# A decoder layer on one core: every on-chip tile is moved to byte 0 of a 256-byte line

## The chip, the cores and the metric

The kernel runs on one core of one Trainium2 chip. Its time is the device time of one execution in microseconds. The kernel before took 1461.62 us (median of 3 runs, 1461.08 to 1461.69).

## The reference

One decoder layer for 512 tokens of 1024 features, in float32:

```
x <- x + 1/2 * SwiGLU(RMSNorm(x))                       first FFN, 1024 -> 2 x 2816 -> 1024
h  = RMSNorm(x);  P = h @ W_in                          one projection for all mixers
branch A: sparse attention, 16 heads x 64 (compressed, selected, sliding window)
branch B: short gated convolution, 1024 channels
branch M: cross-attention into 256 memory tokens, 4 heads x 256
x <- x + W_out( sig(gA)*A + sig(gB)*B + sig(gM)*M )
x <- x + 1/2 * SwiGLU(RMSNorm(x))                       second FFN, same shapes
```

With 512 tokens every key block is selected and the window holds all earlier tokens, so the two large branches of A are causal attentions over 512 keys.

## The kernel before, in words

Activations stand as features on the 128 partitions and tokens on the free axis. Every product is done in float32r with both operands split exactly into two parts, hi and lo; `mm3` (L194 to L199) issues three matmuls for each product of tiles, at L197 (hi, hi), L198 (hi weights, lo activations) and L199 (lo weights, hi activations). Each matmul loads a stationary operand of 128 columns (512 bytes per partition) and streams a moving operand, in most cases of 512 columns (2048 bytes per partition).

Weights come from DRAM in units of up to 128x1024 float32 (`Weights`, from L58): SyncE issues a load into one of three `wraw` buffers, ScalarE rounds a half into `whi` (L93), VectorE takes the rest into `wlo` (L94), each with two buffers, one unit ahead of the use.

The stages follow each other on TensorE:

- First FFN (`ffn`, L258 to L309), in three groups of 8, 7 and 7 blocks of 128 hidden features. Each group first does its up-projections (two units per block, each 8 x 3 = 24 matmuls: stationary `whi` or `wlo`, moving `Ahi` or `Alo`, out to PSUM `psg` and `pso`), then its down-projection (8 units of 24 or 21 matmuls: stationary `whi`/`wlo`, moving `ghi`/`glo`, out to `pss`). So an up group has 8 x 48 = 384 or 7 x 48 = 336 long matmuls, a down group 192 or 168.
- Keys and values of the memory (`mem_kv`): 192 long matmuls, stationary `mhi`/`mlo`, moving `whi`/`wlo`.
- Token-major projections (`tok_chunk`, `stage_b`): stationary `Ahi`/`Alo`, moving `whi`/`wlo`, 512 columns wide in six chunks of 96 matmuls, 304 and 256 wide in two more, with the compression and the attention over the memory set between them. In the latter (`mem_head`) the values `Vm` are stationary and the probabilities `mph`/`mpl` move, twelve matmuls in a row per head.
- Eight rounds (`feat_quanta`, `att_quanta`), each 144 long matmuls for the convolution and the merge gates (stationary `whi`/`wlo`, moving `Ahi`/`Alo`), in bursts of nine, and between the bursts the transposes, scores and value products of the attention.
- The output projection (`tail`, L1161 on): 192 long matmuls, moving `Ahi`/`Alo`; then the second FFN through the same `ffn`, with `x2hi`/`x2lo` in place of `Ahi`/`Alo`.

The program is written in this order; the order of the instructions on each engine comes from the order of the closures that `interleave` (L44) sets among each other. On-chip memory is taken from pools, stacked from the left or the right end; in a pool each tile starts where the one before it ended, rounded up to 32 bytes. So where a tile begins follows from the sizes of those ahead of it: `small` (412 bytes) begins at byte 128 of a 256-byte line, and what follows it is shifted by what remains. In the built program the tiles that TensorE reads begin at these bytes (the address per partition, and its remainder by 256):

| Tile | Before: address, byte in line | After: address, byte in line |
|---|---|---|
| Ahi; Alo | 33856, 64; 50240, 64 | 34304, 0; 50688, 0 |
| whi (two buffers) | 80224, 96; 84320, 96 | 80640, 0; 84736, 0 |
| wlo (two buffers) | 88416, 96; 92512, 96 | 88832, 0; 92928, 0 |
| ghi; glo, first FFN | 107936, 160; 124320, 160 | 108544, 0; 124928, 0 |
| mhi; mlo | 168640, 192; 176832, 192 | 168192, 0; 176384, 0 |
| Vm (first); mph, heads 0 and 1 | 204768, 224; 188384, 224 | 204544, 0; 188160, 0 |
| V2; PThi (first) | 154784, 160; 204640, 96 | 155392, 0; 204032, 0 |
| x2hi; x2lo | 96608, 96; 112992, 96 | 97024, 0; 113408, 0 |
| ghi; glo, second FFN | 137568, 96; 153952, 96 | 137984, 0; 154368, 0 |

Slices of these tiles that a long matmul reads lie whole multiples of 512 bytes from the tile's start, so the remainder by 256 is the same for all of a tile's matmuls.

Of the kernel before, what the change touches and what calls it, by code (L numbers as in the profile page):

```python
# [11 lines left out]
F32 = mybir.dt.float32  # L12
# [12 lines left out]
EPS = 1e-6  # L25
NEG8 = -8e30
TW = 528
WL = 656
BUCKET_START = (0, 1, 2, 3, 4, 5, 6, 7, 8, 9, 10, 11, 12, 13, 14, 15,
                16, 19, 21, 24, 27, 31, 35, 40, 46, 52, 59, 67, 77, 87, 99, 113)  # L30
RAW_BUFS = 3
LOOK = 1

# columns of the per-feature constants
# [3 lines left out]
# chunks of projections with tokens on partitions: columns, and k tiles of each unit  # L38
# [5 lines left out]
def interleave(main, aux):  # L44
    """Emit the closures of aux evenly between those of main."""
    n, done = len(main), 0
    for i, fn in enumerate(main):
        fn()
        want = (i + 1) * len(aux) // n
        while done < want:  # L50
            aux[done]()
            done += 1
    while done < len(aux):
        aux[done]()
        done += 1


class Weights:  # L58
    """Streams weight units from DRAM and splits them exactly into two float32r parts."""
# [18 lines left out]
    def _half(self):  # L78
        """Split one half of the next unit."""
        j = self.i_split  # L80
        t, n = self.raw[j]
        if j not in self.parts:
            hi = self.pool.tile([128, 1024], F32R, tag="whi", name=f"whi{j}", bufs=LOOK + 1)
            lo = self.pool.tile([128, 1024], F32R, tag="wlo", name=f"wlo{j}", bufs=LOOK + 1)
            self.parts[j] = (hi, lo)
            c = slice(0, min(n, 512))
        else:
            c = slice(512, n)
        if c.stop == n:
            self.raw.pop(j)  # L90
            self.i_split += 1
        hi, lo = self.parts[j]
        self.nc.scalar.copy(hi[:, c], t[:, c])  # L93
        self.nc.vector.tensor_sub(lo[:, c], t[:, c], hi[:, c].bitcast(F32))  # L94
        self.prefetch()
# [5 lines left out]
    def use(self, key):  # L101
        """The next unit; its key must be the one expected here. Begins to split the one after it."""
        assert self.units[self.i][1] == key, (self.units[self.i][1], key)
        self.prefetch()
        while self.i_split <= self.i:
            self._half()
        self.i += 1
        self.ahead()
        return self.parts[self.i - 1]

    def ahead(self):
        """Split another half of the unit after the one in use (called in the middle of a unit)."""
        self.parts.pop(self.i - 2, None)
        if self.i_split < len(self.units) and self.i_split <= self.i + LOOK - 1:
            self._half()


class Layer:
    def __init__(self, ctx, tc, ins, out, dbg=None):
# [3 lines left out]
        self.per = ctx.enter_context(tc.tile_pool(name="per", bufs=1, side="left"))  # L123
        self.wp = ctx.enter_context(tc.tile_pool(name="wp", bufs=1, side="left"))
        self.psum = ctx.enter_context(tc.tile_pool(name="ps", bufs=2, space=bass.MemoryType.PSUM))
        self.dram = ctx.enter_context(tc.tile_pool(name="dr", bufs=1, space=bass.MemoryType.DRAM))
        self.ws = Weights(nc, self.wp, self.unit_list())

# [65 lines left out]
    def mm3(self, ps, ahi, alo, bhi, blo, start, stop):  # L194
        """ps (+)= a.T @ b, each operand in its two exact parts."""
        mm = self.nc.tensor.matmul
        mm(ps, ahi, bhi, start=start, stop=False)  # L197
        mm(ps, ahi, blo, start=False, stop=False)  # L198
        mm(ps, alo, bhi, start=False, stop=stop)  # L199

    def rsqrt(self, pool, v, n, out, p=128):
        """out = v ** -0.5 over [p, n]: an estimate from the exponent bits, then Newton's steps."""
# [10 lines left out]
    def rstd(self, pool, ssq, n, width, out):  # L213
        """out = rsqrt(ssq / width + EPS) over [128, n]."""
# [4 lines left out]
    def token_rstd(self, pool, acc, nb, out):  # L219
        """acc [128 features, 128*nb tokens], squares already summed over feature tiles -> out [128 tok, nb]."""  # L220
        p = self.ps("t")
# [4 lines left out]
    def bcast_rows(self, rs, R):  # L226
        """R[m, t] = rs[t] for every partition m; rs is [128 tok, 4]."""
# [5 lines left out]
    def split_scaled(self, hi, lo, src, scale):  # L233
        """hi, lo = the exact parts of src * scale (scale per partition)."""
# [7 lines left out]
    def prep_post(self, pool, k, src, gcol, hi, lo, acc):  # L242
        """Parts of src * gain for a product scaled by rstd afterwards, and the running sum of squares."""
# [3 lines left out]
    def square_sum(self, pool, k, src, acc):  # L247
        """acc (+)= src ** 2"""
# [9 lines left out]
    def ffn(self, key, pool, xhi, xlo, R, done, before, extra=()):  # L258
        """done(m, ps): takes the last partial product (times 4 of what is to be added to x).
        before(): emitted after the first two products, which do not need R; extra: closures  # L260
        emitted one by one after the following ones."""
# [50 lines left out]
    def run(self):  # L312
# [20 lines left out]
        # the engines' first use, while the first loads run  # L333
# [11 lines left out]
        for h in (1, 0):  # L345
            mkp[h] = memkv[h].enter_context(tc.tile_pool(name=f"mkp{h}", bufs=1, side="right"))
        prep = ExitStack()
        pp = prep.enter_context(tc.tile_pool(name="pp", bufs=1, side="right"))
        f1 = ExitStack()
        fp = f1.enter_context(tc.tile_pool(name="fp", bufs=1, side="left"))  # L350

        # first ffn
# [24 lines left out]
        # h = rmsnorm(x1), under the product of the memory's keys and values  # L377
# [15 lines left out]
        # mixing phase  # L393
        mx1 = ExitStack()
        self.m1 = mx1.enter_context(tc.tile_pool(name="m1", bufs=1, side="left"))
# [8 lines left out]
    def bias_table(self, pool):  # L404
# [18 lines left out]
        def repeat(h, n):  # L423
            # a head's row once per query of a block, so that a pitch of WL - 1 shifts it by one
# [25 lines left out]
    def mem_kv(self, pools, pp, aux):  # L450
        """Emits the product; returns the closures that finish the keys."""
# [64 lines left out]
    def tok_chunk(self, c, evac):  # L516
        """Closures for one chunk of columns; evac(tb, ps) takes each block of 128 tokens."""
# [21 lines left out]
    def stage_b(self, memkv, prep, kfin):  # L539
# [7 lines left out]
        # inputs of the compression, while the memory's keys are finished  # L547
        kcs = ExitStack()
        kcv = kcs.enter_context(tc.tile_pool(name="kcs", bufs=1, side="left")).tile([128, 4, 512], F32, name="kcv")
# [5 lines left out]
        cp = cs.enter_context(tc.tile_pool(name="cp", bufs=1, side="right"))  # L555
# [30 lines left out]
        # keys and values of the selected and the window branch, with the memory's attention  # L586
        self.mx2 = ExitStack()
        m2 = self.mx2.enter_context(tc.tile_pool(name="m2", bufs=1, side="left"))
# [3 lines left out]
        pool = ma.enter_context(tc.tile_pool(name="ma0", bufs=1, side="right"))  # L592
# [5 lines left out]
        kp = kx.enter_context(tc.tile_pool(name="kp", bufs=1, side="left"))  # L598
# [26 lines left out]
        pool = ma.enter_context(tc.tile_pool(name="ma1", bufs=1, side="right"))  # L625
# [5 lines left out]
        # queries  # L631
        self.rx = ExitStack()
        self.tp = self.rx.enter_context(tc.tile_pool(name="tp", bufs=1, side="right"))
# [43 lines left out]
        # the first heads' scores, under the last chunk of queries  # L677
        self.rp = self.rx.enter_context(tc.tile_pool(name="rp", bufs=1, side="right"))
# [23 lines left out]
    def key_parts(self, dst, src):  # L702
        """dst rows 0..63 the high, rows 64..127 the low parts of the keys (src holds them in both halves)."""
# [12 lines left out]
    def compress(self, cp, kcv, kind):  # L716
# [7 lines left out]
        def trans(gp):  # L724
# [6 lines left out]
            # token = 16 * c + 2 * q + parity  # L731
# [93 lines left out]
    def mem_heads(self, pool, qtok, mrsq, heads):  # L825
        """Closures of the heads' attention, each head's second half among the next one's first."""
# [12 lines left out]
    def mem_head(self, pool, qtok, mrsq, h):  # L839
# [19 lines left out]
        def score(i2):  # L859
            if i2 == 0:  # L860
                st["P"] = pool.tile([128, 4, 256], F32, tag="mP", name=self.nm("mP"))
                st["sum"] = pool.tile([128, 4], F32, tag="msum", name=self.nm("msum"))
                st["nm"] = pool.tile([128, 4], F32, tag="mnm", name=self.nm("mnm"))
# [14 lines left out]
        def norm():  # L878
            r = pool.tile([128, 4], F32, tag="mr", name=self.nm("mr"))
# [29 lines left out]
    def q_norm(self, h):  # L909
        """The head's normalised queries, twice side by side."""  # L910
# [21 lines left out]
    def softmax_part(self, s, T, P, nm, ssum):  # L932
        """P = exp(score - max), its sum in ssum; the score is s / 8 + T / 8."""
# [39 lines left out]
    def probs(self, b, part):  # L973
        """Scale by gate / sum, in two parts."""
# [32 lines left out]
    def pv(self):  # L1007
        """The product of the last transposed block with its values."""
# [38 lines left out]
    def combine(self):  # L1047
        """Add the two halves of a finished head's output: rows 0..63 the main, 64..127 the low part."""
# [112 lines left out]
    def tail(self, mx1):  # L1161
# [12 lines left out]
        fp = f2.enter_context(tc.tile_pool(name="fp2", bufs=1, side="left"))  # L1174
# [35 lines left out]
def layout(i):  # L1210
    """The arrays as the kernel reads them: elements moved and copied, nothing computed from them."""
# [4 lines left out]
    def feat(w, n):  # L1216
        """[128 p, k * 128 + col] blocks of a [K, 128 * n] matrix."""
# [3 lines left out]
    def tok(w):  # L1221
        """Units of two k tiles and 512 columns of a [1024, 512 * n] matrix."""
# [3 lines left out]
    def units(w, kts):  # L1226
        """Units of some k tiles each of a [1024, n] matrix, side by side on 128 partitions."""
# [57 lines left out]
```

## Time and profile before

| What | Value |
|---|---|
| Time, median of 3 runs | 1461.62 us |
| Span of the profiled execution | 1460.0 us |
| TensorE (PE) busy | 1448.8 us, 99% |
| VectorE (DVE) busy | 888.6 us, 61% |
| ScalarE (ACT) busy | 633.5 us, 43% |
| DMA engines, mean in the first FFN and in the rounds | 0.37 and 0.24 of their time |

The profile shows each matmul with a start and a modelled end. Matmuls overlap: a long one is shown with some 390 to 400 ns, while the next begins some 230 ns after it. What TensorE needs for a stretch of matmuls is therefore read from starts: the length of a stretch in which it never idles, divided by the matmuls in it. A stretch's count includes those that reach into it from before. Times below count from the span's start.

### The profile page before, as it was taken

How to read it: one execution, taken by the hardware profiler on the slowest of the kernel's cores; microseconds unless marked ns; L12 is line 12 of the kernel's file. 1: busy time of each engine (PE TensorE's matmuls, PEld its weight loads, DVE VectorE, ACT ScalarE, POOL GpSimd, SP SyncE). 2: the span in 40 equal slices, each digit the busy share in tenths (PEclk: the TensorE clock that was granted, in tenths of full speed). 3: DMA queues.
4: the chain of work that ended last, by engine and by line, in shares of the span. 5: the costliest groups of instructions: out<-in, count | busy, mean ns of one | idle time of the engine just before them, and what ended most of it. 6: DMA issues, size and time to landing. Idle time of an engine off the chain costs nothing.

```text
span 1460.0 us, 18864 instructions
## 1 busy us (share of the span) xinstructions
PE 1448.8 (99%) x6915; PEld 1199.6 (82%) x6915; DVE 888.6 (61%) x2120; ACT 633.5 (43%) x1455; POOL 1.3 (0%) x8
## 2 busy tenths in 40 slices
PE   9999999999999999999999999999999999999998
PEld 7788888888887789878888888888888888888887
DVE  6463544454676566688777787877755444454553
ACT  5241322233555555565566566556533222322321
POOL 0000000000000000000000000000000000000000
PEclk9999999999999999999999999999999999999999
DMA  5733233333452421222222222221233332333332
GB/s 178 245 119 102 87 96 92 102 85 90 138 178 75 149 93 57 89 80 66 88 66 75 76 69 73 70 84 58 72 102 87 101 94 95 101 90 100 99 92 96
DMA packets 42892, 142.62 MB, mean 98 GB/s; under 512 B 4704, under 2 KB 4992, under 8 KB 42672
## 3 DMA queue, kind: packets, MB, share of 16 engines
q1 hardware_dynamic: 40320, 134.83, 29.8%
q10 hardware_dynamic: 2480, 6.60, 1.3%
q8 instruction: 54, 0.88, 0.2%
q14 instruction: 38, 0.31, 0.1%
HBM read 139.27 MB, written 7.51 MB: 101 GB/s over the span
## 4 chain that ended last, share of the span: by engine, by line
PE 96%; DVE 2%; ACT 1%; issue 1%; DMA 0%; SPq 0%; ACTq 0%
PE psg L197 15%; PE psg L198 15%; PE psg L199 15%; PE pso L197 7%; PE pso L199 7%; PE pso L198 7%; PE pss L198 6%; PE pss L199 6%; PE pss L197 6%; PE pst L1001 2%; PE pss L959 1%; PE pso L1025 1%; PE pss L958 1%; PE pso L1024 1%; PE pst L926 1%
## 5 line engine op out<-in xcount | busy, mean ns | idle before, releaser
L93 ACT CAST whi<-wraw 128x512 fp32r<-128x512 f32 (+1 forms) x492 | 280.2, 611 | 576.9 <-issue 334.4
L94 DVE TENSOR_TENSOR wlo<-wraw,whi 128x512 fp32r<-128x512 f32 (+1 forms) x492 | 315.4, 675 | 70.3 <-ACT whi L93 69.4
L197 PE MATMUL psg<-Ahi,whi 128*128 128x512 f32 x624 | 250.2, 401 | 0.7 <-ACT Ahi L235 0.6
L198 PE MATMUL psg<-Alo,whi 128*128 128x512 f32 x624 | 247.0, 396 | 1.1 <-DVE Alo L236 1.1
L199 PE MATMUL psg<-Ahi,wlo 128*128 128x512 f32 x624 | 246.7, 395 | 0.0
L199 PEld LDWEIGHTS psg<-Ahi,wlo 128*128 128x128 f32 x624 | 117.2, 188 | 27.6
L198 PEld LDWEIGHTS psg<-Alo,whi 128*128 128x128 f32 x624 | 117.4, 188 | 25.4 <-DVE Alo L236 2.4
L197 PEld LDWEIGHTS psg<-Ahi,whi 128*128 128x128 f32 x624 | 117.4, 188 | 25.1 <-ACT Ahi L235 1.5
L199 PE MATMUL pss<-ghi,wlo 128*128 128x512 f32 x352 | 137.9, 392 | 0.0
L197 PE MATMUL pss<-ghi,whi 128*128 128x512 f32 x352 | 137.8, 391 | 0.0
L198 PE MATMUL pss<-glo,whi 128*128 128x512 f32 x352 | 137.6, 391 | 0.0
L935 ACT ACTIVATE P<-P,nm 128x128 f32<-128x128 f32 (+3 forms) x128 | 72.2, 564 | 81.8 <-DVE nm L934 81.8
L278 DVE TENSOR_TENSOR fa<-psg,R 128x512 f32<-128x512 f32 x44 | 30.4, 692 | 123.9 <-PE psg L199 121.1
L294 DVE TENSOR_TENSOR fa<-fa,pso 128x512 f32<-128x512 f32 x44 | 30.3, 688 | 90.1 <-PE pso L199 90.1
L307 DVE SCALAR_TENSOR_TENSOR xT<-pss,xT 128x512 f32<-128x512 f32 x32 | 22.1, 692 | 102.2 <-PE pss L199 102.2
L239 ACT CAST PThi<-pst 128x512 fp32r<-128x512 f32 (+3 forms) x128 | 54.6, 426 | 61.5 <-PE pst L1001 61.2
L198 PEld LDWEIGHTS pss<-glo,whi 128*128 128x128 f32 x352 | 66.2, 188 | 14.4
L199 PEld LDWEIGHTS pss<-ghi,wlo 128*128 128x128 f32 x352 | 66.2, 188 | 14.3
L197 PEld LDWEIGHTS pss<-ghi,whi 128*128 128x128 f32 x352 | 66.2, 188 | 14.1
L240 DVE TENSOR_TENSOR PTlo<-pst,PThi 128x512 fp32r<-128x512 f32 (+3 forms) x128 | 62.4, 487 | 22.5 <-ACT PThi L239 22.3
L934 DVE CUSTOM_DVE_ANT_0 P<-pss,T 128x128 f32<-128x128 f32 (+3 forms) x128 | 62.1, 485 | 18.3 <-PE pss L959 18.2
L199 PE MATMUL pso<-Ahi,wlo 128*128 128x512 f32 x176 | 69.7, 396 | 0.0
(280 smaller groups left out, 2749.2 us busy)
## 6 DMA issues: line engine op xcount, KB each, us to landing
wraw<-wfeat SPq DMA_DIRECT2D x48, 512.0 KB, 3.4
wraw<-wf2i SPq DMA_DIRECT2D x44, 512.0 KB, 3.6
wraw<-wf1i SPq DMA_DIRECT2D x43, 512.0 KB, 3.6
wraw<-wmkv SPq DMA_DIRECT2D x16, 512.0 KB, 3.5
wraw<-wf1o SPq DMA_DIRECT2D x16, 448.0 KB, 3.3
wraw<-wf2o SPq DMA_DIRECT2D x16, 448.0 KB, 3.3
scr<-scr ACTq DMA_DIRECT2D x1, 5248.0 KB, 25.1
T<-scr SPq DMA_DIRECT2D x16, 264.0 KB, 3.4
```

What stands on the lines that cost most here:

```text
L93: self.nc.scalar.copy(hi[:, c], t[:, c])
L94: self.nc.vector.tensor_sub(lo[:, c], t[:, c], hi[:, c].bitcast(F32))
L197: mm(ps, ahi, bhi, start=start, stop=False)
L198: mm(ps, ahi, blo, start=False, stop=False)
L199: mm(ps, alo, bhi, start=False, stop=stop)
L239: self.nc.scalar.copy(hi, src)
L240: self.nc.vector.tensor_tensor(lo, src, hi.bitcast(F32), op=ALU.subtract)
L278: nc.vector.tensor_tensor(a, p, R, op=ALU.mult)
L294: nc.vector.tensor_tensor(a, a, p2, op=ALU.mult)
L934: self.nc.vector.tensor_tensor_reduce(P, s, T, -0.125, 3.0e38, ALU.add, ALU.min, nm)
L935: self.nc.scalar.activation(P, P, AF.Exp, scale=-1.0, bias=nm, accum_out=ssum)
L1001: nc.tensor.transpose(p[:, (i - j) * 128:(i - j + 1) * 128], P[:, o:o + 128], self.ident)
```

## The change

Pools are wrapped in a class `Aligned`. A tile whose size is a multiple of 256 bytes is taken as before; a float32 tile under 256 bytes with one buffer becomes a slice of a shared 256-byte line of its pool (slices begin at multiples of 32 bytes); any other tile is rounded up to whole lines. One unused tile at each end of the memory (128 bytes left, 224 bytes right) shifts the pools so that all of them begin at a multiple of 256. In the attention over the memory, the small tiles `msum`, `mnm` and `mr` are taken from the pool `m1` and no longer from the head's own pool. Everything else in the diff is comments taken out.

```
+LINE = 256
+PAD_LEFT, PAD_RIGHT = 128, 224
...
+class Aligned:
+    def __init__(self, pool):
+        self.pool, self.slots, self.line, self.used, self.n = pool, {}, None, LINE, 0
+
+    def tile(self, shape, dtype, name=None, tag=None, bufs=1):
...
+        size = 4 * n
+        if size % LINE == 0:
+            return self.pool.tile(shape, dtype, name=name, tag=tag or name, bufs=bufs)
+        if size < LINE and bufs == 1 and dtype == F32:
+            key = tag or name
+            if key not in self.slots:
+                need = (size + 31) // 32 * 32
+                if self.used + need > LINE:
...
+                    self.line, self.used = self.pool.tile([128, LINE // 4], F32, name=label, tag=label), 0
+                self.slots[key] = (self.line, self.used // 4)
+                self.used += need
+            line, at = self.slots[key]
+            t = line[:shape[0], at:at + n]
+        else:
+            m = (size + LINE - 1) // LINE * (LINE // 4)
+            t = self.pool.tile([shape[0], m], dtype, name=name, tag=tag or name, bufs=bufs)[:, :n]
...
-        self.per = ctx.enter_context(tc.tile_pool(name="per", bufs=1, side="left"))
-        self.wp = ctx.enter_context(tc.tile_pool(name="wp", bufs=1, side="left"))
+        for side, pad in (("left", PAD_LEFT), ("right", PAD_RIGHT)):
+            shift = ctx.enter_context(tc.tile_pool(name="shift_" + side, bufs=1, side=side))
+            shift.tile([128, pad // 4], F32, name="shift_" + side)
+        self.per = self.pool(ctx, "per", "left")
+        self.wp = self.pool(ctx, "wp", "left")
...
+    def pool(self, stack, name, side):
+        return Aligned(stack.enter_context(self.tc.tile_pool(name=name, bufs=1, side=side)))
...
-                st["sum"] = pool.tile([128, 4], F32, tag="msum", name=self.nm("msum"))
-                st["nm"] = pool.tile([128, 4], F32, tag="mnm", name=self.nm("mnm"))
+                st["sum"] = self.m1.tile([128, 4], F32, tag="msum", name=self.nm("msum"))
+                st["nm"] = self.m1.tile([128, 4], F32, tag="mnm", name=self.nm("mnm"))
```

Instruction by instruction, the five engines' programs of the changed kernel are those of the kernel before, in the same order, with the same shapes; only names and addresses of tiles differ. The waits are the same but for four in one place: ScalarE's exponentials of one memory head (L875) also wait for earlier instructions of ScalarE itself, since their sums lie in a line that is used again.

## Rows read from the trace of the kernel before

**Rows 1.** Page, part 1: busy time, share, instructions; part 4: engines on the chain.
```profile
PE 1448.8 (99%) x6915; PEld 1199.6 (82%) x6915; DVE 888.6 (61%) x2120; ACT 633.5 (43%) x1455; POOL 1.3 (0%) x8
...
PE 96%; DVE 2%; ACT 1%; issue 1%; DMA 0%; SPq 0%; ACTq 0%
```

**Rows 2.** TensorE's waits: line, whom it waited for, total us, times, longest.
```profile
PE psg L197 <- ACT whi L93: 1.7, 2, 1.2
```

**Rows 3.** Groups by shape, 146.54 to 225.30 (first FFN): busy us, mean ns.
```profile
L197 PE MATMUL psg<-Ahi,whi 128*128 128x512 f32 x56 | 22.1, 396 | 0.0
...
L240 DVE TENSOR_TENSOR glo<-fa,ghi 128x512 fp32r<-128x512 f32 x6 | 4.1, 683 | 0.0
L239 ACT CAST ghi<-fa 128x512 fp32r<-128x512 f32 x6 | 3.7, 617 | 0.0
```

**Rows 4.** The same view, 1227.45 to 1303.62 (second FFN).
```profile
L197 PE MATMUL psg<-x2hi,whi 128*128 128x512 f32 x56 | 21.8, 389 | 0.0
...
L240 DVE TENSOR_TENSOR glo<-fa,ghi 128x512 fp32r<-128x512 f32 x6 | 4.1, 688 | 0.0
L239 ACT CAST ghi<-fa 128x512 fp32r<-128x512 f32 x6 | 3.7, 615 | 0.0
```

**Rows 5.** Stretches: length, busy us and count by engine; PEclk, DMA share, GB/s.
```profile
core 0: us, PE busy (x) PEld busy (x) DVE busy (x) ACT busy (x) POOL busy (x), PEclk, DMA share, GB/s
22.00:101.74 79.74, 79.74 (x341) 63.24 (x340) 48.73 (x92) 29.56 (x59) 0.00 (x0) 1.00 0.52 175
101.74:146.54 44.80, 44.80 (x193) 36.29 (x192) 15.73 (x25) 9.68 (x18) 0.00 (x0) 1.00 0.30 95
146.54:225.30 78.76, 78.76 (x341) 63.47 (x340) 39.19 (x63) 23.11 (x42) 0.00 (x0) 1.00 0.31 91
225.30:263.85 38.55, 38.55 (x170) 31.64 (x170) 16.31 (x37) 8.61 (x18) 0.00 (x0) 1.00 0.34 102
263.85:342.25 78.40, 78.40 (x338) 63.12 (x337) 39.04 (x62) 22.77 (x41) 0.00 (x0) 1.00 0.31 91
342.25:380.70 38.45, 38.45 (x169) 31.55 (x168) 18.43 (x31) 12.79 (x24) 0.00 (x0) 1.00 0.32 101
390.00:425.00 35.00, 35.00 (x153) 28.02 (x152) 31.36 (x68) 26.12 (x59) 0.00 (x0) 1.00 0.58 183
1050.00:1090.00 40.00, 40.00 (x175) 32.04 (x174) 23.79 (x39) 16.86 (x31) 0.00 (x0) 1.00 0.31 93
1183.93:1227.45 43.52, 43.52 (x193) 36.04 (x192) 15.76 (x25) 9.69 (x18) 0.00 (x0) 1.00 0.33 97
1227.45:1303.62 76.17, 76.17 (x338) 63.06 (x337) 39.04 (x62) 22.75 (x41) 0.00 (x0) 1.00 0.32 94
1303.62:1341.69 38.07, 38.07 (x169) 31.53 (x168) 14.82 (x25) 8.95 (x18) 0.00 (x0) 1.00 0.35 101
700.00:1040.00 340.00, 340.00 (x1792) 287.64 (x1791) 269.35 (x850) 200.95 (x559) 0.00 (x0) 1.00 0.23 73
```

**Rows 6.** TensorE in order of time, a memory head's value products: start us, shown us.
```profile
545.95 0.40 PE L197 MATMUL pss<-mph,Vm 128*128 128x512 f32 x1
...
547.81 0.39 PE L199 MATMUL pss<-mph,Vm 128*128 128x512 f32 x1
...
548.49 0.39 PE L199 MATMUL pss<-mph,Vm 128*128 128x512 f32 x1
```

**Rows 7.** The same view, second FFN, after the transposes of L230.
```profile
1111.13 0.40 PE L197 MATMUL psg<-x2hi,whi 128*128 128x512 f32 x1
...
1113.21 0.39 PE L197 MATMUL pso<-x2hi,whi 128*128 128x512 f32 x1
...
1114.80 0.39 PE L198 MATMUL pso<-x2lo,whi 128*128 128x512 f32 x1
```

**Rows 8.** The same view, one burst of nine in a round.
```profile
802.81 0.40 PE L198 MATMUL psg<-Alo,whi 128*128 128x512 f32 x1
...
804.68 0.40 PE L1024 MATMUL pso<-PThi,V 128*128 128x512 f32 x1
```

**Rows 9.** ScalarE in order of time: a memory head's exponential and its sum.
```profile
544.41 0.48 ACT L875 ACTIVATE mP<-pss,mnm 128x256 f32<-128x256 f32 x1
544.78 0.20 ACT L875 ACTIVATION_READ_ACCUMULATOR mP<-pss,mnm 128x1 f32 x1
```

More of the change, by code (lines that the diff above doesn't have):

```diff
@@ L55, in interleave @@
         done += 1
+class Aligned:
+    def __init__(self, pool):
+        self.pool, self.slots, self.line, self.used, self.n = pool, {}, None, LINE, 0
+    def tile(self, shape, dtype, name=None, tag=None, bufs=1):
+        n = 1
+        for d in shape[1:]:
+            n *= d
+        size = 4 * n
[6 more added lines that the diff above has]
+                if self.used + need > LINE:
+                    self.n += 1
+                    label = f"line{self.n}_{self.pool.name}"
+                    self.line, self.used = self.pool.tile([128, LINE // 4], F32, name=label, tag=label), 0
[6 more added lines that the diff above has]
+            t = self.pool.tile([shape[0], m], dtype, name=name, tag=tag or name, bufs=bufs)[:, :n]
+        if len(shape) == 2:
+            return t
+        names = [f"d{i}" for i in range(len(shape) - 1)]
+        return t.rearrange("p (" + " ".join(names) + ") -> p " + " ".join(names),
+                           **{k: v for k, v in zip(names[1:], shape[2:])})
 class Weights:
@@ L345, in run @@
         for h in (1, 0):
-            mkp[h] = memkv[h].enter_context(tc.tile_pool(name=f"mkp{h}", bufs=1, side="right"))
+            mkp[h] = self.pool(memkv[h], f"mkp{h}", "right")
         prep = ExitStack()
-        pp = prep.enter_context(tc.tile_pool(name="pp", bufs=1, side="right"))
+        pp = self.pool(prep, "pp", "right")
         f1 = ExitStack()
-        fp = f1.enter_context(tc.tile_pool(name="fp", bufs=1, side="left"))
+        fp = self.pool(f1, "fp", "left")
         acc = fp.tile([128, 512], F32, tag="acc", name="acc1")
@@ L394, in run @@
         mx1 = ExitStack()
-        self.m1 = mx1.enter_context(tc.tile_pool(name="m1", bufs=1, side="left"))
+        self.m1 = self.pool(mx1, "m1", "left")
         self.OM = self.m1.tile([128, NK, S], F32, name="OM")
@@ L548, in stage_b @@
         kcs = ExitStack()
-        kcv = kcs.enter_context(tc.tile_pool(name="kcs", bufs=1, side="left")).tile([128, 4, 512], F32, name="kcv")
+        kcv = self.pool(kcs, "kcs", "left").tile([128, 4, 512], F32, name="kcv")
         def clear():
@@ L554, in stage_b @@
         prep.close()
-        cp = cs.enter_context(tc.tile_pool(name="cp", bufs=1, side="right"))
+        cp = self.pool(cs, "cp", "right")
         mssq = m1.tile([128, 4, 4], F32, name="mssq")
@@ L587, in stage_b @@
         self.mx2 = ExitStack()
-        m2 = self.mx2.enter_context(tc.tile_pool(name="m2", bufs=1, side="left"))
+        m2 = self.pool(self.mx2, "m2", "left")
         self.K2 = [m2.tile([128, 4, 544], F32R, name="K2s"), m2.tile([128, 4, 512], F32R, name="K2w")]
@@ L591, in stage_b @@
         ma = ExitStack()
-        pool = ma.enter_context(tc.tile_pool(name="ma0", bufs=1, side="right"))
+        pool = self.pool(ma, "ma0", "right")
         interleave(v[8:], [mstd] + self.mem_heads(pool, mtok, mrsq, (0, 1)))
@@ L597, in stage_b @@
         kx = ExitStack()
-        kp = kx.enter_context(tc.tile_pool(name="kp", bufs=1, side="left"))
+        kp = self.pool(kx, "kp", "left")
         ktok = kp.tile([128, 2, 4, 256], F32, name="ktok")
@@ L624, in stage_b @@
         ma = ExitStack()
-        pool = ma.enter_context(tc.tile_pool(name="ma1", bufs=1, side="right"))
+        pool = self.pool(ma, "ma1", "right")
         interleave(self.tok_chunk("s", evac_k(0)) + self.tok_chunk("w", evac_k(1)),
@@ L632, in stage_b @@
         self.rx = ExitStack()
-        self.tp = self.rx.enter_context(tc.tile_pool(name="tp", bufs=1, side="right"))
+        self.tp = self.pool(self.rx, "tp", "right")
         self.T = {h: self.load_T(h) for h in range(2)}
@@ L675, in stage_b @@
         kx.close()
-        self.rp = self.rx.enter_context(tc.tile_pool(name="rp", bufs=1, side="right"))
+        self.rp = self.pool(self.rx, "rp", "right")
         self.Pc = self.rp.tile([128, 4, 128], F32, name="Pc")
@@ L878, in norm @@
         def norm():
-            r = pool.tile([128, 4], F32, tag="mr", name=self.nm("mr"))
+            r = self.m1.tile([128, 4], F32, tag="mr", name=self.nm("mr"))
             nc.vector.reciprocal(r, st["sum"])
@@ L1173, in tail @@
         f2 = ExitStack()
-        fp = f2.enter_context(tc.tile_pool(name="fp2", bufs=1, side="left"))
+        fp = self.pool(f2, "fp2", "left")
         xhi = fp.tile([128, NK, S], F32R, name="x2hi")
```

## The prediction

> **What bounds the kernel.** I read the page's busy times and its chain first [rows 1]. TensorE is busy for 1448.8 of 1460.0 us and makes up 96% of the chain that ended last; VectorE has 61%. Its largest single wait is 1.7 us in two pieces [rows 2]. So the time is the number of matmuls times the distance from one start to the next, and a change that moves no instruction can only act through that distance. The granted clock is 1.00 in every stretch [rows 5], the upper level of 2.4 GHz, so the clock explains no difference below.
>
> Next I set two equal pieces of work side by side. An up group of seven blocks is 336 long matmuls, by the same lines of code, in both FFNs. In the first FFN it takes 78.40 us, in the second 76.17 [rows 5]: 233.3 and 226.7 ns from start to start. The groups by shape say the same: 56 matmuls of one line show 396 ns each in the first, 389 in the second [rows 3, 4]. Shape, PSUM tiles, the weight buffers, ScalarE's and VectorE's work beside them (39.04 us of VectorE in both) and the DMA share (0.31, 0.32) agree. What differs is where the moving operand begins. By the table of addresses `whi` and `wlo` begin at byte 96 of a 256-byte line in both; `Ahi`/`Alo` begin at 64, `x2hi`/`x2lo` at 96. The down groups repeat it: in the second FFN `ghi` is at 96 too and 192 matmuls take 43.52 us (226.7 each); in the first it is at 160, and they take 44.80 (233.3), 38.55 and 38.45 for the groups of 168 (229.5 and 228.9) [rows 5].
>
> It is the relation of the two operands, not the place of one. In the memory's keys and values the moving `whi` is at 96 as `x2hi` is, but the stationary `mhi` at 192: 35.00 us hold 148 long starts and four transposes, about 234.5 each [rows 5]. In the value products of a memory head both operands are at 224. There the first eight starts are 1.86 us, 232.5 ns, apart, the next three 0.68 us, 226.7 each [rows 6]. The second FFN behaves the same after a break: nine starts over 2.08 us (231.1), then seven over 1.59 (227.1) [rows 7]. So two streams with equal remainders slide against each other for eight or nine matmuls, settle at 226.7 ns, and stay there; with unequal remainders they settle at 229 to 234.5.
>
> **The change part by part.** No instruction is removed, added or moved; on all five engines the order is the same. What changes is that all operands of all long matmuls get equal remainders, 0. I take 226.7 ns as the settled distance, since every stream of equal remainders in this trace has it, and the difference to 233.3, 6.6 ns, as the gain of a settled long matmul.
>
> - First FFN, up groups. The third goes from 78.40 to 76.17: 2.2 us. The second (78.76) contains four small matmuls more, which stay: 2.2. Of the first, 79.74 us run steadily [rows 5], and 2.8% of them are 2.3; I take 2.1, since streams must settle after its early breaks. Sum 6.5.
> - First FFN, down groups: 44.80 - 43.52 = 1.3, 38.55 - 38.07 = 0.5, 38.45 - 38.07 = 0.4 [rows 5]. Sum 2.2.
> - Memory's keys and values: 192 x (234.5 - 226.7) = 1.5, less one settling: 1.4.
> - Output projection: the stretch from 1050 runs at about 233 ns (175 in 40.00 us, a few of them short) [rows 5]; 192 x 6.6 = 1.3, taken as 1.2.
> - Token-major projections: 576 long matmuls at unequal remainders, at most 576 x 6.6 = 3.8. Transposes and scores break the stream, so I take half, 1.8; the lower end is 0.5.
> - Rounds: 1152 long matmuls in bursts of nine. One burst shows eight starts over 1.87 us, 233.8 ns [rows 8]. A stream of equal remainders needs eight or nine matmuls to settle and runs at 231.1 to 232.5 meanwhile [rows 6, 7], so a burst may be over as it settles: 1.3 ns each gives 1.5 us, full settling 7.6. I take 2.0, near the settling rows.
> - Shorter matmuls, value products and scores of the attention: 0.4; I have no row of equal remainders at their widths, so 0 to 1.5.
> - Second FFN: remainders were equal and stay equal: 0.
>
> ScalarE and VectorE I cost at nothing: with tiles at other remainders in the two FFNs, `glo` took 683 and 688 ns, `ghi` 617 and 615 [rows 3, 4]. In the rounds VectorE is busy for 269 of 340 us [rows 5]; 2% faster matmuls leave it room. The four added waits of ScalarE on itself stand before exponentials; behind each are the next exponential, the accumulator read and the evacuations of that head, and the transposes of TensorE that follow wait for these. At most each costs one accumulator read, 0.20 us [rows 9], 0.8 in all; ScalarE works in order, the earlier instruction is mostly done by then, and other matmuls stand between, so I take 0. Loads land at other bytes; TensorE waits for them only in the first microseconds, and I take 0.
>
> Sum: 6.5 + 2.2 + 1.4 + 1.2 + 1.8 + 2.0 + 0.4 = 15.5 us off the profiled span of 1460.0, so 1444.5. The median of the runs lies 1.6 above that span, so 1446.1; I write 1446. With the ends of the unknown terms (settling in the rounds and the token-major part at its best or at nothing) this case alone reaches from 1438 to 1450.
>
> **The rivals.**
>
> - *Nothing happens, since lines of 256 bytes are not what counts.* All pairs of equal remainder by 256 that the trace has are equal by 512 too (`x2hi` 96608 and `whi` 80224 differ by 32 x 512). After the change `whi` (80640) and `Ahi` (34304) differ by an odd multiple of 256, and so do `whi` and the first `ghi`. If the pattern of the two streams repeats only after 512 bytes, the first FFN, the token-major part, the rounds and the output projection gain nothing, and only the memory's 1.4 us remain, as `mhi` and `whi` then agree by 512 too: 1460. For it: no row excludes it. Against it: differences of 32, 64 and 96 bytes already give different distances, 233.3, 229 to 233 and 234.5, so the pattern is fine-grained. The Trainium skill speaks for no effect at all: "SBUF — State Buffer", section "Who interferes with whom", says that TensorE never waits on anyone for SBUF, and "TensorE: Matmul & The Clock Gate", section "Step-by-step: what each phase is for", that loading weights takes no read bandwidth from the running matmul, as each has its own port. By that rule addresses do not matter and the time stays at 1461.6; the 396 against 389 ns of the same instruction [rows 3, 4] speak against it. Chance 0.18.
> - *More is gained.* Byte 0 may suit both streams better than 96 or 224, which are both 32 bytes into a 64-byte piece, and the second FFN would fall as well. If long matmuls lost a further 6.6 ns in both FFNs, the memory and the output projection (1584 + 1584 + 192 + 192 = 3552), that is 23.4 us more: 1423. For it, only that no such pair stands in the trace. Against it: with one operand at 64, that is on such a boundary, and the other not, the distance is 233.3 whichever it is. Chance 0.08.
> - *Slower.* Two streams that both begin at byte 0 could collide where those at 32 bytes past a boundary pass each other. Then the second FFN, the only large part now at 226.7, would lose it: 1584 x 6.6 = 10.5 us, the two first-FFN down groups now at 229 would go to 233.3 (336 x 4.2 = 1.4), nothing would be gained elsewhere: 1461.6 + 11.9 = 1473. It decides as soon as an equal pair at byte 0 does not settle under 230 ns. For it: equal pairs are known at bytes 96 and 224 alone. Against it: those two agree, though `wraw`, `whi`, `wlo`, `x2hi`, `acc` and `R` all share byte 96 in the second FFN without harm. Chance 0.12.
>
> **How the numbers follow.** The forecast has 0.62. A measurement of this kernel can tell about 0.2%, 2.9 us, from no change. Forecast and larger gain lie beyond that on the fast side: 0.70, and a little of the no-change rival, if half the pairs settle, makes it 0.71. No change keeps 0.17, slower 0.12. The range goes from 1436, just past the forecast's own end, to 1463, which holds the no-change case; outside are the larger gain and the slower case, 0.20 together.
>
> **What would show it.** Right: the up groups of the first FFN show 389 ns per matmul and take 76.2 us, those of the second FFN stay; the rounds shrink by 1 to 4 us; ScalarE's and VectorE's durations stay. Wrong: 396 ns remains in the first FFN (no change), the second FFN's falls below 385 (more), or rises to 396 (slower). A new wait of TensorE over 2 us would mean that a cost I set to nothing was one.

## The result

The changed kernel takes 1444.9 us (median of 4 runs, 1444.43 to 1445.15) where the kernel before takes 1461.42 in the same measurement: a ratio of 0.9886, 95% interval 0.9872 to 0.9900. The profiled execution's span fell from 1460.0 to 1443.4 us, by 16.6. The forecast was 1446 with 15.5 us gained.

Part 1 of the page and the chain, of the changed kernel; they answer to [rows 1].

```profile
PE 1431.8 (99%) x6915; PEld 1198.8 (83%) x6915; DVE 887.8 (62%) x2120; ACT 631.5 (44%) x1455; POOL 1.3 (0%) x8
...
PE 97%; DVE 1%; ACT 1%; DMA 0%; issue 0%; SPq 0%; ACTq 0%
```

TensorE's busy time fell by 17.0 us with the same 6915 matmuls; VectorE's and ScalarE's moved by 2 us at most (888.6 to 887.8, 633.5 to 631.5), nor did the weight loads beside the matmuls (1199.6 to 1198.8). So TensorE's time fell by far the most, and with the same matmuls that means the distance between them.

The groups by shape of the second up group of the first FFN in the changed kernel, 143.28 to 219.80 us (columns as in [rows 3]):

```profile
L240 PE MATMUL psg<-Ahi,whi 128*128 128x512 f32 x56 | 21.8, 389 | 0.0
...
L283 DVE TENSOR_TENSOR glo<-fa,ghi 128x512 fp32r<-128x512 f32 x6 | 4.1, 685 | 0.0
L282 ACT CAST ghi<-fa 128x512 fp32r<-128x512 f32 x6 | 3.7, 614 | 0.0
```

The matmul went from 396 to the 389 ns that the second FFN had before [rows 3, 4]; `glo` and `ghi` kept theirs (683 and 617).

Stretches of the changed kernel, which answer to [rows 5]: the first FFN's second to sixth groups, then two groups of the second FFN.

```profile
core 0: us, PE busy (x) PEld busy (x) DVE busy (x) ACT busy (x) POOL busy (x), PEclk, DMA share, GB/s
99.76:143.28 43.52, 43.52 (x193) 36.04 (x192) 15.75 (x25) 9.66 (x18) 0.00 (x0) 1.00 0.32 97
143.28:219.80 76.52, 76.52 (x341) 63.42 (x340) 39.19 (x63) 23.05 (x42) 0.00 (x0) 1.00 0.31 93
219.80:258.03 38.23, 38.23 (x171) 31.62 (x170) 16.30 (x37) 8.60 (x18) 0.00 (x0) 1.00 0.35 101
258.03:334.19 76.16, 76.16 (x338) 63.06 (x336) 39.02 (x62) 22.71 (x41) 0.00 (x0) 1.00 0.32 95
334.19:372.27 38.08, 38.08 (x170) 31.53 (x168) 18.42 (x31) 12.74 (x24) 0.00 (x0) 1.00 0.33 102
1167.31:1210.83 43.52, 43.52 (x193) 36.04 (x192) 15.75 (x25) 9.69 (x18) 0.00 (x0) 1.00 0.32 97
1210.83:1286.99 76.16, 76.16 (x337) 63.06 (x336) 39.03 (x62) 22.71 (x41) 0.00 (x0) 1.00 0.32 94
```

The first FFN's groups now take what the second's take: 76.16 us for 336 matmuls, 43.52 for 192, 226.7 ns each. (Its second up group, 76.52, contains four small matmuls more.) To see where all 16.6 us came from, the whole span is cut at the same places of the program. The kernel before (first FFN, memory's keys and values, token-major part, rounds with output projection, second FFN to the end):

```profile
5.84:380.70 374.86, 373.12 (x1605) 299.25 (x1604) 190.33 (x331) 118.72 (x220) 0.00 (x0) 1.00 0.38 119
380.70:427.08 46.38, 46.38 (x206) 37.35 (x204) 39.43 (x88) 31.35 (x68) 0.00 (x0) 1.00 0.53 172
427.08:647.32 220.24, 215.76 (x1180) 183.17 (x1179) 141.19 (x371) 121.00 (x289) 0.56 (x2) 1.00 0.29 94
647.32:1095.32 448.00, 448.00 (x2311) 376.75 (x2310) 345.60 (x1044) 259.06 (x695) 0.00 (x0) 1.00 0.24 75
1095.32:1460.00 364.68, 360.78 (x1597) 298.31 (x1595) 170.60 (x283) 100.20 (x181) 0.00 (x0) 1.00 0.32 96
```

The changed kernel:

```profile
6.12:372.27 366.15, 364.52 (x1606) 298.76 (x1604) 189.93 (x330) 118.01 (x219) 0.00 (x0) 1.00 0.39 121
372.27:417.37 45.10, 45.10 (x205) 37.24 (x204) 39.05 (x88) 31.08 (x68) 0.00 (x0) 1.00 0.54 175
417.37:636.13 218.76, 213.78 (x1181) 183.63 (x1180) 140.97 (x371) 120.61 (x289) 0.56 (x2) 1.00 0.30 95
636.13:1078.72 442.59, 442.59 (x2312) 375.85 (x2310) 345.55 (x1045) 258.16 (x695) 0.00 (x0) 1.00 0.24 76
1078.72:1443.40 364.68, 360.75 (x1597) 298.31 (x1595) 170.51 (x283) 100.03 (x181) 0.00 (x0) 1.00 0.32 96
```

Within the fourth line of each, the output projection alone, before and after; what is left of the line belongs to the rounds:

```profile
1050.06:1095.32 45.26, 45.26 (x197) 36.27 (x195) 26.81 (x43) 18.83 (x34) 0.00 (x0) 1.00 0.31 94
1034.55:1078.72 44.17, 44.17 (x198) 36.13 (x196) 26.84 (x43) 18.79 (x34) 0.00 (x0) 1.00 0.30 96
```

| Stage | Forecast | Measured (before - after) |
|---|---|---|
| First FFN | 8.7 | 374.86 - 366.15 = 8.7 |
| Memory's keys and values | 1.4 | 46.38 - 45.10 = 1.3 |
| Token-major part | 1.8 | 220.24 - 218.76 = 1.5 |
| Rounds, with the attention's short matmuls | 2.0 + 0.4 = 2.4 | 402.74 - 398.42 = 4.3 |
| Output projection | 1.2 | 45.26 - 44.17 = 1.1 |
| Second FFN | 0 | 364.68 - 364.68 = 0.0 |
| Ahead of the first long matmul | 0 | 5.84 - 6.12 = -0.3 |

The last row says little: in the traces of the experiments below the first long matmul begins anywhere from 5.36 to 6.22 us. In the token-major part TensorE's busy time fell by 2.0 us (215.76 to 213.78) and its idle time rose by 0.5.

### The profile page after: what moved, and what is told of

It reads as the page before. It is cut to its first block, busy times and chain, and to the rows that moved or that the text cites. A ratio compares the mean times of both kernels' runs of the same rounds, so it can differ in the third digit from the quotient of the medians.

```text
span 1443.4 us, 18864 instructions
## 1 busy us (share of the span) xinstructions
PE 1431.8 (99%) x6915; PEld 1198.8 (83%) x6915; DVE 887.8 (62%) x2120; ACT 631.5 (44%) x1455; POOL 1.3 (0%) x8
## 4 chain that ended last, share of the span: by engine, by line
PE 97%; DVE 1%; ACT 1%; DMA 0%; issue 0%; SPq 0%; ACTq 0%
PE psg L240 15%; PE psg L241 15%; PE psg L242 15%; PE pso L240 8%; PE pso L242 8%; PE pso L241 8%; PE pss L241 6%; PE pss L242 6%; PE pss L240 6%; PE pst L1044 2%; PE pso L1068 1%; PE pss L1002 1%; PE pss L1001 1%; PE pso L1067 1%; PE pst L969 1%; DMA xT<-xT 0%
## 5 line engine op out<-in xcount | busy, mean ns | idle before, releaser
L242 PE MATMUL psg<-Ahi,wlo 128*128 128x512 f32 x624 | 243.8, 391 | 0.0
L240 PEld LDWEIGHTS pss<-ghi,whi 128*128 128x128 f32 x352 | 66.1, 188 | 13.6
```

## The experiments

Theory: the distance between long matmuls hangs on the difference between the addresses of the moving operand and of the stationary one; it settles at 226.7 ns where they agree by 256 bytes. Rivals: a tile must itself begin at byte 0; the gain came by another engine or by loads; the pattern is another than one of 256 bytes. All kernels compute the whole layer.

**All tiles at byte 32.** The changed kernel with other pads:

```
-PAD_LEFT, PAD_RIGHT = 128, 224
+PAD_LEFT, PAD_RIGHT = 160, 192
```

> The changed kernel with both pads 32 bytes further: every tile begins at byte 32 of its 256-byte line, so all pairs of operands keep equal remainders and no tile begins on a line. Theory (the distance between two long matmuls hangs on the difference of the two operands' addresses): 226.7 ns settled everywhere, 1445 us, within 1 us of the changed kernel's 1444.9. Rival (tiles must begin at byte 0 of a line): the gain goes, 1461 us.

Measured: 1444.91 us (4 runs), ratio to the kernel before 0.9886 (0.9872 to 0.9901), the changed kernel's own ratio. The third up group of the first FFN and the second of the second FFN:

```profile
257.83:333.99 76.16, 76.16 (x337) 63.06 (x336) 39.02 (x62) 22.71 (x41) 0.00 (x0) 1.00 0.32 95
1210.48:1286.64 76.16, 76.16 (x338) 63.08 (x336) 39.02 (x62) 22.71 (x41) 0.00 (x0) 1.00 0.31 94
```

Both take 76.16 us, as at byte 0. No tile begins on a line here, and nothing is lost: the line's start does not matter. In the kernel before, pairs at byte 96 and at byte 224 had the same distance.

**Only Ahi and Alo moved, in the kernel before.** `xT`, which stands ahead of them, moves with them.

```
+        per.tile([128, 8], F32, name="ahead")
         self.xT = per.tile([128, NK, S], F32, name="xT")
...
+        per.tile([128, 56], F32, name="behind")
         self.gates = per.tile([128, 4, 48], F32, name="gates")
```

> The kernel before with one thing changed: 32 bytes ahead of xT and 224 behind Alo put Ahi and Alo at byte 96, where whi and wlo stand; everything else keeps its remainder. Theory: the up groups of the first FFN (6.6 us), the output projection (1.2), the token-major projections and the rounds (some 5) gain; down groups of the first FFN and the memory's keys and values do not: about 1448.6 us (1447 to 1451), up groups at 226.7 ns. Rival (byte 0 counts): 1461 us, up groups at 233.3 ns.

Measured: 1447.71 us (4 runs), ratio 0.9906 (0.9892 to 0.9921). Its first down group, its third up group, and its memory's keys and values:

```profile
99.14:143.10 43.96, 43.96 (x193) 36.05 (x192) 15.72 (x25) 9.68 (x18) 0.00 (x0) 1.00 0.32 96
258.23:334.41 76.18, 76.18 (x337) 63.06 (x336) 39.04 (x62) 22.68 (x41) 0.00 (x0) 1.00 0.32 94
372.88:419.27 46.39, 46.39 (x205) 37.36 (x204) 39.41 (x88) 31.27 (x68) 0.00 (x0) 1.00 0.53 172
```

Two unused tiles of 256 bytes together bring 13.6 of the 16.5 us, with the operands at byte 96. The up group is at 226.7 ns; the memory's keys and values, whose operands were not touched, keep their 46.38 us of before. One group gained against the expectation: the first down group, whose operands both lie 256 bytes further on and so differ as before (by 64 in the remainder), takes 43.96 us (229.0 ns each) and took 44.80 (233.3) [rows 5]. So at 64 bytes the distance depends on something besides the difference of addresses; the scans below meet both values again.

**Only Ahi and Alo moved back, in the changed kernel.** A short line of 224 bytes ahead of `xT` and 32 bytes behind `zero` put `xT`, `Ahi`, `Alo`, `gates` and `zero` at byte 224:

```
-        self.ones = per.tile([128, 1], F32, name="ones")
+        line = per.pool.tile([128, 56], F32, name="short_line")
+        self.ones = line[:, 0:1]
...
-        warm = per.tile([128, 1], F32, name="warm")
+        warm = line[:, 8:9]
...
+        per.pool.tile([128, 8], F32, name="back")
```

> The changed kernel with Ahi and Alo alone moved back to a difference of -32 bytes from whi and wlo, as before (byte 224 against byte 0); xT and gates move with them. Theory: the up groups of the first FFN return to 233.3 ns, and the rounds, the token-major part and the output projection lose what they gained, the rest keeps its gain: about 1457.5 us (1455 to 1459). Rival (other tiles of the change, VectorE, ScalarE or loads, brought the gain): under 1450 us.

Measured: 1457.71 us (10 runs), ratio 0.9975 (0.9966 to 0.9985): 12.8 us lost again. A down group and an up group of the first FFN, and an up group of the second:

```profile
101.73:145.26 43.53, 43.53 (x193) 36.05 (x192) 15.74 (x25) 9.65 (x18) 0.00 (x0) 1.00 0.32 97
262.21:340.62 78.41, 78.41 (x338) 63.13 (x337) 39.00 (x62) 22.71 (x41) 0.00 (x0) 1.00 0.32 92
1223.75:1299.91 76.16, 76.16 (x338) 63.06 (x337) 39.02 (x62) 22.70 (x41) 0.00 (x0) 1.00 0.32 94
```

The up group that reads `Ahi` is back at 78.41 us; the groups that do not keep 43.5 and 76.16. All tiles but these five keep their places of the change, and VectorE, ScalarE and the DMA engines are as busy beside the slow up group as beside the fast one (39.00, 22.71 us and 0.32 against 39.02, 22.71 and 0.32). So neither VectorE, ScalarE nor the loads made that part of the gain.

**Which differences settle.** Four kernels move four tiles to other bytes, one per stage, while the weights stay at 0. Each uses this helper, with the offsets that its expectation names:

```
+def shifted(pool, shape, dtype, off, name, tag=None):
+    n = shape[1] * shape[2]
+    t = pool.pool.tile([128, n + 64], dtype, name=name, tag=tag or name, bufs=1)
+    return t[:, off // 4:off // 4 + n].rearrange("p (a b) -> p a b", b=shape[2])
...
-        xhi = fp.tile([128, NK, S], F32R, name="x2hi")
+        xhi = shifted(fp, [128, NK, S], F32R, 32, "x2hi")
```

> The changed kernel with four tiles at other bytes while the weights stay at 0: ghi/glo of the first FFN at 128, x2hi/x2lo at 32, ghi/glo of the second FFN at 192, mhi/mlo (stationary) at 16. Read per stage, settled ns from start to start. Theory with a pattern of 256 bytes: difference 128 somewhere from 229 to 235, 32 gives 233.3, 192 (that is -64) 229 to 233.3, -16 unknown, above 226.7. Pattern of 128 bytes: 128 gives 226.7, 192 as 64. Rival (only byte 0 counts): all four alike, above 226.7. About 1463 us in all (second FFN +8, first down groups +2 to +3).

> As the first scan, with ghi/glo of the first FFN at 64, x2hi/x2lo at 160, ghi/glo of the second FFN at 224, mhi/mlo at 128. Theory with a pattern of 256 bytes: 64 gives 229 to 233.3, 160 (-96) about 234, 224 (-32) 233.3, -128 as 128 in the first scan. With a pattern of 128 bytes: 160 as 32 (233.3), 224 as 96 (234), -128 gives 226.7.

> As the first scan, with ghi/glo of the first FFN at 96, x2hi/x2lo at 128, ghi/glo of the second FFN at 16, mhi/mlo at 64. Theory: 96 gives about 234; 128 the same in the up groups of the second FFN as in the down groups of the first scan; 16 tells the grain: 226.7 if pieces of 32 bytes count, above if smaller ones do; -64 229 to 233.3.

> As the first scan, with ghi/glo of the first FFN at 16, x2hi/x2lo at 64, ghi/glo of the second FFN at 8, mhi/mlo at 192. Theory: 64 settles at 229 to 233.3 as in the first FFN before; 16 the same in this stage as 16 in the third scan; 8 bytes is two columns of the moving operand: near 226.7 if pieces of 16 bytes or more count, above if not.

In one run each they took 1459.13, 1458.28, 1457.55 and 1456.61 us. What is read is single groups: 192 matmuls of a down group or 336 of an up group. First scan (difference 128, then 32, then 192):

```profile
99.16:143.96 44.80, 44.80 (x194) 36.04 (x193) 15.72 (x25) 9.69 (x18) 0.00 (x0) 1.00 0.31 95
...
1218.13:1296.54 78.41, 78.41 (x338) 62.98 (x336) 39.00 (x62) 22.69 (x41) 0.00 (x0) 1.00 0.31 91
1173.34:1218.13 44.79, 44.79 (x193) 36.10 (x192) 15.74 (x25) 9.70 (x18) 0.00 (x0) 1.00 0.32 94
```

Second scan (64, 160, 224):

```profile
99.44:143.40 43.96, 43.96 (x193) 36.06 (x192) 15.74 (x25) 9.68 (x18) 0.00 (x0) 1.00 0.32 96
1216.62:1295.33 78.71, 78.71 (x337) 63.28 (x336) 39.01 (x62) 22.70 (x41) 0.00 (x0) 1.00 0.32 91
1171.82:1216.62 44.80, 44.80 (x194) 36.09 (x192) 15.73 (x25) 9.70 (x18) 0.00 (x0) 1.00 0.31 94
```

Third scan (96, 128, 16):

```profile
99.18:144.00 44.82, 44.82 (x194) 36.05 (x193) 15.73 (x25) 9.67 (x18) 0.00 (x0) 1.00 0.31 95
1217.71:1295.79 78.08, 78.08 (x338) 63.30 (x336) 39.01 (x62) 22.70 (x41) 0.00 (x0) 1.00 0.31 92
1173.23:1217.71 44.48, 44.48 (x193) 36.10 (x192) 15.72 (x25) 9.69 (x18) 0.00 (x0) 1.00 0.32 95
```

Fourth scan (64, then 8):

```profile
1215.57:1293.97 78.40, 78.40 (x337) 63.51 (x336) 38.99 (x62) 22.69 (x41) 0.00 (x0) 1.00 0.30 91
1170.77:1215.57 44.80, 44.80 (x193) 36.80 (x192) 15.73 (x25) 9.68 (x18) 0.00 (x0) 1.00 0.32 94
```

The memory's keys and values move `whi`/`wlo`, at 0, past the stationary `mhi`/`mlo`, at 16, 128, 64 and 192 in the four scans. Their last 96 matmuls, one line per scan:

```profile
398.83:421.23 22.40, 22.40 (x98) 18.14 (x96) 19.52 (x48) 15.36 (x37) 0.00 (x0) 1.00 0.59 188
...
396.98:419.30 22.32, 22.32 (x98) 18.09 (x96) 19.54 (x48) 15.35 (x37) 0.00 (x0) 1.00 0.62 189
...
399.10:421.50 22.40, 22.40 (x98) 17.95 (x97) 19.52 (x48) 15.34 (x37) 0.00 (x0) 1.00 0.59 188
...
398.24:420.21 21.97, 21.97 (x97) 18.03 (x96) 19.56 (x48) 15.27 (x37) 0.00 (x0) 1.00 0.62 196
```

Length by count gives the mean settled distance for each difference, the moving operand's byte less the stationary one's, by 256:

| Difference, bytes | Distance, ns |
|---|---|
| 0 (whole multiples of 256, odd and even ones) | 226.7 |
| 8 | 233.3 |
| 16 | 231.7 |
| 32 | 233.4 |
| 64 | 229.0 in the down group, 228.9 in the memory's part, 233.3 in the up group |
| 96 | 233.4 |
| 128 | 233.3, 232.4, and 232.5 in the memory's part |
| 160 | 234.3 |
| 192 (-64) | 233.3, also in the memory's part |
| 224 (-32) | 233.3 |
| 240 (-16) | 233.3, in the memory's part |

Of the differences tried only 0 settles at 226.7: not 128, so the pattern is not one of 128 bytes, and not 8, so two columns are enough to lose it. That a difference of 256 is as good as 0 is shown by the changed kernel itself: `whi` (80640) and `Ahi` (34304) differ by an odd multiple of 256 there, and its up group takes 76.16 us. The forks in the expectations are decided by this: the pattern is one of 256 bytes, and pieces of 8 bytes count. Two were missed: a difference of 128 was to give the same wherever it stands, and gives 232.4 to 233.3, and the first scan took 1459.13 us, not 1463. The rival that all differences but 0 are alike fell too, since they reach from 228.9 to 234.3 ns. With 64 giving two values, the difference alone does not fix the distance where it is not 0.

**One load in three apart.** `wlo`, like the tiles behind it, stays at byte 0, with `Ahi`, `Alo` and `whi` at 224; the edit is the third experiment's, with its 32 bytes set between `whi` and `wlo`:

```
-        per.pool.tile([128, 8], F32, name="back")
...
+            if j == 0:
+                self.pool.pool.tile([128, 8], F32, name="back")
             lo = self.pool.tile([128, 1024], F32R, tag="wlo", name=f"wlo{j}", bufs=LOOK + 1)
```

> The changed kernel with xT, Ahi, Alo, gates, zero, wraw and whi at byte 224 and everything else, wlo with it, at byte 0. In the up groups of the first FFN one load of weights in three (wlo, loaded while the matmul of L198 streams Alo) differs from the moving operand, by 32 bytes; in the second FFN, where x2hi, x2lo, ghi and glo are at 0, two in three (whi) differ. Theory that the load running beside a matmul delays it, pair by pair: the mean distance is 226.7 + 6.6/3 = 228.9 ns in the first FFN's up groups and 226.7 + 2 x 6.6/3 = 231.1 in the second's. Rival (the whole stream must agree to settle): 233.3 in both. About 1452 us in all for the first, 1460 for the second.

Measured: 1471.74 us in one run, beside 1461.7 of the kernel before. An up group of each FFN, and the whole second FFN to the end:

```profile
264.16:342.54 78.38, 78.38 (x338) 63.02 (x337) 39.00 (x62) 22.76 (x41) 0.00 (x0) 1.00 0.30 92
1230.70:1309.11 78.41, 78.41 (x338) 63.06 (x337) 39.04 (x62) 22.73 (x41) 0.00 (x0) 1.00 0.31 91
...
1094.89:1470.00 375.11, 371.18 (x1597) 298.27 (x1595) 170.61 (x283) 100.15 (x181) 0.00 (x0) 1.00 0.31 93
```

The mean distance is 233.3 ns (78.38 by 336) in the first FFN, where one load in three differs, and 233.4 (78.41 by 336) in the second, where two in three do. The theory of a price per pair, 228.9 and 231.1, fell; the rival's 233.3 came in both. A stream with one load in three apart by 32 bytes gains nothing. The rival's total, 1460 us, was missed all the same: it leaves no room for what the second FFN loses, which stood at 226.7 ns before. That takes 375.11 us here and 364.68 in the kernel before, and this is about the 10 us by which the kernel is slower. It comes near the slower rival (1473), reached by another way.

## Why the prediction was right

- *The bound.* The step from chain and busy times to "a change of addresses can only act through the distance between matmuls" held: 17.0 us less of TensorE, at unchanged loads, VectorE and ScalarE.
- *The relation, not the place.* This was the step on which the sum rested, and the three timed experiments show it: equal remainders at byte 32 give all of the gain, at byte 96 the part that hangs on `Ahi`, and undoing that part alone loses 12.8 us.
- *226.7 ns as the settled distance at byte 0.* Right: 76.16 us by 336. So the rival "more" fell; byte 0 and byte 32 are the same. One argument against it was misread: with one operand on a 64-byte boundary the rows have 233.3 where it is the moving one, but 234.5 in the memory's part, where it is the stationary one. The rival "slower" fell by the same rows: the second FFN takes 364.68 us before and after.
- *First FFN, memory, token-major part.* 8.7, 1.3 and 1.5 against 8.7, 1.4 and 1.8. For the token-major part the forecast was half of a bound, taken without a row; that it came out so near is luck.
- *Rounds.* This term was too small: with the short matmuls, which no row had and which the stretches do not set apart, 4.3 us against 2.4, where the sign to look for was a fall of 1 to 4. The output projection came as forecast, 1.1 against 1.2. In the rows on settling after a break [rows 6, 7] eight or nine matmuls ran at 231 to 232.5 ns; the bursts of the changed kernel run faster. One burst's starts, which answer to [rows 8]:

```profile
802.57 0.40 PE L241 MATMUL psg<-Alo,whi 128*128 128x512 f32 x1
...
804.40 0.39 PE L1067 MATMUL pso<-PThi,V 128*128 128x512 f32 x1
...
805.42 0.40 PE L240 MATMUL psg<-Ahi,whi 128*128 128x512 f32 x1
...
807.47 0.33 PE L1067 MATMUL pso<-PThi,V 128*128 128x384 f32 x1
```

  Eight starts take 1.83 us (228.8 ns) in this burst and nine take 2.05 (227.8) in the next, where I had reckoned with 231 to 232.5 from two samples. Why these bursts settle sooner is not shown; what ran before them may matter.
- *No change.* This rival had the best case against the forecast, that equality by 512 might be needed; the changed kernel and the scans show that 256 is enough and 128 is not. The Trainium skill's rule that went with it, in "SBUF — State Buffer", section "Who interferes with whom", is that TensorE never waits on anyone for SBUF. The time that was read from it, an unchanged 1461.6, did not come: the same instruction takes 226.7 or 233.3 ns by the difference of its own two operands' addresses. Whether that is a wait at SBUF, and so whether the rule itself fails, no run here shows.
- *Costs set at nothing.* TensorE's idle time is 11.6 us of the span (1443.4 less 1431.8), 11.2 before, and its largest wait is 1.7 us in two pieces, the longer 1.2, as before [rows 2]:

```profile
PE psg L240 <- ACT whi L130: 1.7, 2, 1.2
```

  ScalarE's exponential with the added wait starts as close behind the accumulator read as without it: the read at 535.34 is shown 0.19 us, and the next exponential begins 0.09 after its start, as at the same place in the kernel before (546.09 and 546.18).

```profile
535.34 0.19 ACT L918 ACTIVATION_READ_ACCUMULATOR mP<-pss,line_m 128x1 f32 x1
535.43 0.46 ACT L918 ACTIVATE mP<-pss,line_m 128x256 f32<-128x256 f32 x1
```

What stays open: in which part of the chip the two streams meet. The rows show that the distance depends on the difference of addresses by 256 bytes, and that at a difference of 0 a stream needs some matmuls after a break until it runs at 226.7 ns. That the streams slide against each other until they no longer meet is a picture for this; no row shows it.

## What to carry to other kernels

Where TensorE streams long float32r matmuls without a gap, compare the distance between starts across stages of equal shape; a few per cent between them at an equal clock can be the addresses. Give the moving and the stationary operand, hi and lo parts alike, the same remainder by 256. Which remainder did not matter among 0, 32, 96 and 224, and one buffer out of step by 32 bytes cost the whole stream its gain. An unused tile of some bytes in the right place does it.

## What the runs showed of the hardware that was not expected

- At the granted clock of 1.00, 2.4 GHz, 226.7 ns are 544 clock periods, 32 more than the 512 columns, and 233.3 ns are 560, 16 more again. The values between are means of unequal distances: read to the nanosecond from the trace's starts, the 228.9 ns of the kernel before are a repeating 226, 229 and 232.
- Where one load in three differs, the distances of the first FFN's up groups repeat as 233, 239 and 228 ns by the same reading. The longest stands beside the load that differs, but the sum of three, 700, is that of a stream with all pairs apart.
- A difference of 64 bytes has two settled distances, 229.0 and 233.3, even in one group with the same code and the same difference (the first down group, 44.80 us before and 43.96 with `Ahi` and `Alo` moved); which one is taken was not found.
